# Weight loads begun on GpSimd's DMA queue in place of SyncE's, in a hybrid decoder layer (DeltaNet, dilated window and differential attention, gated FFN)

## The chip, the cores and the metric

The kernel runs on one core of a Trainium2 chip. A core has five engines with an instruction queue each, worked off in order: TensorE (PE in the profile), VectorE (DVE), ScalarE (ACT), GpSimd (POOL) and SyncE (SP). They wait for each other through semaphores. Sixteen DMA engines move data between device memory and the core's own memory; a transfer is begun by an instruction in the queue of one of the engines. The metric is the device time of one execution in microseconds; less is better.

## What is computed

One layer of a decoder over 2048 tokens of width 1024, in float32. Three mixers share one input projection and one output projection, and a gated FFN follows:

```python
h_proj = x @ w_in                      # columns split over the three mixers
y = concat([gated_delta_net(...),      # 4 heads, short causal conv, chunked recurrence
            dilated_window_attn(...),  # 4 heads, three dilation patterns
            diff_attn(...)])           # 4 heads, two softmax maps, causal over all tokens
x = layer_norm(alpha * x + y @ w_out)
gate, val = split(causal_conv3(x @ w_up))          # 1024 -> 2 * 2752
x = layer_norm(alpha * x + (silu(gate) * val) @ w_down)
```

## The kernel before

The tokens are worked in four blocks of 512. For each block there is a projection for the attentions (A0 to A3 in the order lists), one for the DeltaNet (G0 to G3), an attention block of each kind (d0 to d3, w0 to w3), the DeltaNet's chunks (i, b, p, r), and the FFN with the layer norms (t0, f0 to f3). The order of the jobs in the program is set by three lists at lines 1341 to 1343, and the instructions of all of them are then laid out engine by engine by the compiler framework's scheduler, which models when each will be ready. So the queue in which an instruction stands, and its modelled duration, shape the order of everything around it.

Every dense product is done three times in a 32-bit format with shortened mantissas: x and w are each split into a high part and a remainder, and PE sums high times high, high times remainder and remainder times high (lines 182 to 184; 1131 to 1134 for the rows' products, 628 to 630 for the values). A weight tile of 128 x 1024 thus needs two halves, `whi` and `wlo`. `Dense.weights` (line 117) delivers them, from one of two sources:

- **raw**: the tile is loaded (line 130), ACT casts it to the high part (line 132), and POOL subtracts that from the raw tile (line 133). 137 tiles go this way. Where the same weight is needed for later blocks (`keep` is set with job A1), both halves are then stored to device memory (line 137), 101 tiles.
- **ready-made**: a weight that was kept is loaded as its two halves (line 127), 291 times, that is 582 transfers of 512 KB.

All of these tiles, raw ones included, live in one ring of seven 4 KB slots per partition (`NW` at line 1326; the raw tiles of the last block's end have a pool of their own for their halves). A raw weight takes three slots, a ready-made one two. A load may begin when the slot's former user is done: with raw weights, raw tile k+3 takes the slot of remainder k, and remainder k+2 takes that of high part k, both freed by the last matmul of product k.

All transfers of the program, 2035 of them, are begun on SP in one queue: these loads, the stores of the halves, the mixers' loads (keys `ks` at line 709, window tiles at 890 to 917, chunks at 430 to 489) and all results. On POOL stand, besides the subtractions, the mixers' triangular selects (`affine_select`, lines 816 and 411), splits of squares (350, 352) and a scaling (568).

Of the kernel before, what the change touches and what calls it, by code (L numbers as in the profile page):

```python
# [27 lines left out]
def cast(x):  # L28
    return x.bitcast(F32)
# [71 lines left out]
class Dense:  # L101
# [15 lines left out]
    def weights(self, src, k=KD, m=P, pool=None, key=None):  # L117


        nc = self.nc  # L120
        shape = lambda w: w[:, 0 : k * m].rearrange("p (k m) -> p k m", k=k)
        own = lambda dt, name: shape(self.wp.tile([P, 1024], dt, tag="w", name=name, bufs=NW))
        put = lambda name: shape(pool.tile([P, 1024], F32R, tag=name, name=name)) if pool else own(F32R, name)
        if key in self.kept:
            parts = put("whi"), put("wlo")
            for part, d in zip(parts, self.kept[key]):
                nc.sync.dma_start(out=cast(part), in_=cast(shape(d)))
            return parts
        raw = own(F32, "wraw")
        nc.sync.dma_start(out=raw, in_=src)  # L130
        hi, lo = put("whi"), put("wlo")
        nc.scalar.copy(hi, raw)  # L132
        nc.gpsimd.tensor_tensor(out=lo, in0=raw, in1=hi, op=ALU.subtract)  # L133
        if key is not None and self.keep:
            self.kept[key] = [self.tc.dram_tile([P, 1024], F32R, name=name) for name in ("whi_d", "wlo_d")]
            for part, d in zip((hi, lo), self.kept[key]):
                nc.sync.dma_start(out=cast(shape(d)), in_=cast(part))
        return hi, lo
# [21 lines left out]
    def put(self, n, emit):  # L160

        self.later.append([n, emit])
# [1056 lines left out]
class Banks:  # L1219
# [10 lines left out]
    def own(self):  # L1230
        return self.banks[-1]
# [190 lines left out]
```

## Time and profile before

| what | value |
|---|---|
| time, median of 3 executions | 3292.46 us (3285.46 to 3297.71) |
| the profiled execution | 3287.69 us |
| its span, first to last instruction | 3285.8 us |
| mean granted clock of PE | 0.955 |
| moved by DMA | 701 MB, mean 213 GB/s, 64% of the 16 DMA engines' time |
| begun on SP | 2035 transfers, all on hardware queue 1 |
| raw weight loads | 137, of 512 KB |
| ready-made halves | 582 loads, of 512 KB |

The page gives busy time by engine; a stretch is a window of the span, in microseconds from its start, for which the same is asked. The trace does not name tile numbers, so the raw weights are followed by their order: the k-th load, the k-th cast and the k-th subtraction belong together. "Idle before" in a row is the time in which the engine stood still just ahead of the instruction, with the event that ended it. Rows of an engine with a q (SPq, POOLq) are its sequencer's: issues and waits, which do not count as busy.

### The profile page before, as it was taken

What the parts mean: (1) busy time and instruction counts of PE and PEld (TensorE: products, weight loads), DVE (VectorE), ACT (ScalarE), POOL (GpSimd) and SP (SyncE); (2) the same over time, 40 slices, a digit from 0 to 9 for tenths busy, and PEclk for the clock granted to TensorE, in tenths of its full rate; (3) what the DMA queues carried; (4) which work ended last, traced back from release to release, by engine and by line L of the source; (5) the groups of instructions that cost most, each with busy time, mean ns of one, the idle gap of its engine ahead of it and who ended that gap; (6) DMA issues with size and microseconds to landing.
All of it is one profiled execution on the core that took longest, in us unless ns stands there. A gap on an engine that the chain in (4) does not pass through costs nothing.

```text
span 3285.8 us, 41437 instructions
## 1 busy us (share of the span) xinstructions
PE 3039.0 (92%) x14476; PEld 2335.1 (71%) x14476; DVE 1940.7 (59%) x3738; ACT 1251.7 (38%) x2735; POOL 493.0 (15%) x342
## 2 busy tenths in 40 slices
PE   7888687999978888998999999999999999999998
PEld 5666576787767667666776667777788666788887
DVE  2564177858544536755887645565897444474446
ACT  2644143353324315644655422232655333221113
POOL 3452252111102003333312000000000000000001
PEclk8899898999988989999999999999999999999999
DMA  6437776766778878766785655555775444665553
GB/s 190 144 132 263 262 257 218 222 208 200 242 253 276 289 246 265 245 225 209 269 281 198 232 187 177 180 184 173 238 261 201 148 162 144 209 236 192 192 188 139
DMA packets 365281, 701.06 MB, mean 213 GB/s; under 512 B 63024, under 2 KB 189488, under 8 KB 364304
## 3 DMA queue, kind: packets, MB, share of 16 engines
q1 hardware_dynamic: 365072, 698.41, 64.0%
q8 instruction: 115, 1.88, 0.2%
q14 instruction: 94, 0.77, 0.1%
HBM read 525.99 MB, written 172.16 MB: 212 GB/s over the span
## 4 chain that ended last, share of the span: by engine, by line
PE 57%; DMA 7%; DVE 4%; ACT 2%; issue 2%; SPq 1%; POOL 0%; ACTq 0%; POOLq 0%; DVEq 0%
PE d L184 9%; PE d L183 9%; PE d L182 9%; PE rp L1131 6%; PE rp L1132 6%; PE rp L1134 5%; PE bank L791 4%; PE bank L806 2%; DMA wraw<-in_w_up 2%; DMA wlo<-wlo_d 2%; PE bank L970 1%; PE bank L740 1%; PE bank L977 1%; PE bank L931 1%; DMA wraw<-in_w_down 1%
## 5 line engine op out<-in xcount | busy, mean ns | idle before, releaser
L182 PE MATMUL d<-xhi,whi 128*128 128x512 f32 x2144 | 872.4, 408 | 54.7 <-DVE i_halo L336 18.1
L184 PE MATMUL d<-xhi,wlo 128*128 128x512 f32 x2144 | 866.4, 404 | 22.4 <-DMA wlo<-wlo_d 18.2
L183 PE MATMUL d<-xlo,whi 128*128 128x512 f32 x2144 | 864.9, 403 | 1.8 <-DVE xlo L145 1.7
L182 PEld LDWEIGHTS d<-xhi,whi 128*128 128x128 f32 x2144 | 416.9, 195 | 164.0 <-issue 20.3
L133 POOL TENSOR_TENSOR wlo<-wraw,whi 128x1024 fp32r<-128x1024 f32 x137 | 337.1, 2461 | 1207.7 <-ACT whi L132 1067.8
L184 PEld LDWEIGHTS d<-xhi,wlo 128*128 128x128 f32 x2144 | 415.9, 194 | 131.8 <-DMA wlo<-wlo_d 20.4
L183 PEld LDWEIGHTS d<-xlo,whi 128*128 128x128 f32 x2144 | 416.6, 194 | 105.8 <-issue 18.2
L1131 PE MATMUL rp<-whi,hhi 128*128 128x512 f32 x704 | 278.6, 400 | 6.0 <-DVE r L1141 2.3
L1132 PE MATMUL rp<-wlo,hhi 128*128 128x512 f32 x704 | 279.3, 397 | 0.0
L1134 PE MATMUL rp<-whi,hlo 128*128 128x512 f32 x672 | 263.0, 397 | 0.0
L132 ACT CAST whi<-wraw 128x1024 fp32r<-128x1024 f32 x137 | 143.6, 1048 | 281.0 <-DMA wraw<-in_w_gdn 65.2
L749 ACT ACTIVATE bank<-bank,nm 128x512 f32<-128x512 f32 (+3 forms) x320 | 190.3, 595 | 110.8 <-DVE nm L745 72.7
L745 DVE TENSOR_REDUCE nm<-bank 128x1 f32<-128x512 f32 (+3 forms) x288 | 165.4, 596 | 72.6 <-PE bank L740 70.4
L1063 ACT COPY ub<-d 128x512 f32<-128x512 f32 x172 | 100.7, 586 | 265.4 <-PE d L184 264.7
L812 DVE SCALAR_TENSOR_TENSOR pd<-pe,f_nlam,pd 128x512 f32<-128x512 f32 (+3 forms) x160 | 123.5, 786 | 124.4 <-ACT pe L808 81.5
L816 POOL TENSOR_SCALAR_AFFINE_SELECT pd<-pd 128x128 f32<-128x128 f32 x64 | 29.8, 472 | 1018.0 <-DVE pd L812 990.6
L1131 PEld LDWEIGHTS rp<-whi,hhi 128*128 128x128 f32 x704 | 133.2, 189 | 43.4 <-issue 6.3
L1132 PEld LDWEIGHTS rp<-wlo,hhi 128*128 128x128 f32 x704 | 133.3, 189 | 35.0 <-issue 8.5
L1141 DVE TENSOR_TENSOR r<-r,rp 128x512 f32<-128x512 f32 x152 | 102.3, 684 | 84.1 <-PE rp L1134 77.4
L1134 PEld LDWEIGHTS rp<-whi,hlo 128*128 128x128 f32 x672 | 127.0, 189 | 33.0 <-issue 6.5
L1064 DVE COPY c_halo<-d 128x2 f32<-128x2 f32 x172 | 26.8, 156 | 205.2 <-ACT ub L1063 205.0
L1068 DVE SCALAR_TENSOR_TENSOR yg<-ub,c_taps,yg 128x512 f32<-128x512 f32 x176 | 144.8, 823 | 3.6
(280 smaller groups left out, 4723.2 us busy)
## 6 DMA issues: line engine op xcount, KB each, us to landing
whi<-whi_d SPq DMA_DIRECT2D x291, 512.0 KB
wlo<-wlo_d SPq DMA_DIRECT2D x291, 512.0 KB
whi_d<-whi SPq DMA_DIRECT2D x101, 512.0 KB
wlo_d<-wlo SPq DMA_DIRECT2D x101, 512.0 KB
ks<-fk_d SPq DMA_DIRECT2D x160, 196.0 KB
wraw<-in_w_up SPq DMA_DIRECT2D x43, 512.0 KB
wraw<-in_w_gdn SPq DMA_DIRECT2D x32, 512.0 KB
wraw<-in_w_down SPq DMA_DIRECT2D x25, 512.0 KB
```

What stands on the lines that cost most here:

```text
L132: nc.scalar.copy(hi, raw)
L133: nc.gpsimd.tensor_tensor(out=lo, in0=raw, in1=hi, op=ALU.subtract)
L182: nc.tensor.matmul(out=ps, lhsT=whi[:, k], rhs=xhi[k], start=(k == 0), stop=False)
L183: nc.tensor.matmul(out=ps, lhsT=whi[:, k], rhs=xlo[k], start=False, stop=False)
L184: nc.tensor.matmul(out=ps, lhsT=wlo[:, k], rhs=xhi[k], start=False, stop=(k == KD - 1))
L745: nc.vector.tensor_reduce(out=o, in_=s[:, 0:nf], axis=mybir.AxisListType.X, op=ALU.min)
L749: nc.scalar.activation(out=s[:, 0:n], in_=s[:, 0:n], func=AF.Exp, scale=-1.0, bias=o, accum_out=den[:, b, m, qt : qt + 1])
L791: nc.tensor.matmul(out=po[64 * hh : 64 * hh + 64, q0:], lhsT=v[:, 64 * hh : 64 * hh + 64], rhs=pd[hh][:, q0:], start=start, stop=stop)
L1068: nc.vector.scalar_tensor_tensor(out=yc, in0=ub[:, j : j + TB], scalar=self.taps[:, mt, j : j + 1], in1=yc, op0=ALU.mult, op1=ALU.add)
L1131: nc.tensor.matmul(out=ps, lhsT=hi[:, sl], rhs=whi, start=first, stop=False)
L1132: nc.tensor.matmul(out=ps, lhsT=hi[:, sl], rhs=wlo, start=False, stop=last and lo is None)
L1134: nc.tensor.matmul(out=ps, lhsT=lo[:, sl], rhs=whi, start=False, stop=last)
```

## The change

Two lines of `Dense.weights` name another engine as the one that begins the transfer. SP keeps the mixers' loads and all stores, the stores of the halves among them.

```diff
         if key in self.kept:
             parts = put("whi"), put("wlo")
             for part, d in zip(parts, self.kept[key]):
-                nc.sync.dma_start(out=cast(part), in_=cast(shape(d)))
+                nc.gpsimd.dma_start(out=cast(part), in_=cast(shape(d)))
             return parts
         raw = own(F32, "wraw")
-        nc.sync.dma_start(out=raw, in_=src)
+        nc.gpsimd.dma_start(out=raw, in_=src)
```

719 of 2035 transfers thus move from SP's queue to POOL's. The scheduler lays out everything anew; the three places below show what the prediction speaks of.

**SP in f0, before.** In the first block of the FFN all weights are raw. `wraw_14377`, `wraw_14420` and `wraw_14470` are three that follow each other; `whi_d` and `wlo_d` are the stores of the halves, `ks` a key tile of the attention.

```order
L137 DMA whi_d_14333<-whi_14329 128x1024
L130 DMA wraw_14377<-in_w_up 128x1024
L137 DMA wlo_d_14334<-wlo_14330 128x1024
L709 DMA ks_9682<-fk_d_1526 98x512
L137 DMA whi_d_14383<-whi_14379 128x1024
L130 DMA wraw_14420<-in_w_up 128x1024
L137 DMA wlo_d_14384<-wlo_14380 128x1024
L137 DMA whi_d_14426<-whi_14422 128x1024
L130 DMA wraw_14470<-in_w_up 128x1024
```

The next raw load stands behind the store of the high part of the weight ahead of it, which needs ACT's cast, and before the store of its remainder, which needs POOL's subtraction.

**POOL at the same place, now.**

```order
L130 DMA wraw_14377<-in_w_up 128x1024
L133 TENSOR_TENSOR wlo_14380<-wraw_14377,whi_14379 128x1024
L130 DMA wraw_14420<-in_w_up 128x1024
L133 TENSOR_TENSOR wlo_14423<-wraw_14420,whi_14422 128x1024
L130 DMA wraw_14470<-in_w_up 128x1024
L133 TENSOR_TENSOR wlo_14473<-wraw_14470,whi_14472 128x1024
```

Load and subtraction alternate; before, the subtractions stood here by themselves. This holds for all raw weights but the last four, with selects of the mixers in between at places. The load of one weight stands behind the subtraction of the weight ahead of it.

**PE at the same place, from the end of the product of `whi_14422` into that of `whi_14472`.** `d` is a product, `bank` an attention score from keys `ks` and queries `qs`. Before:

```order
L182 MATMUL d_14430<-xhi_10799,whi_14422 128x512
L183 MATMUL d_14430<-xlo_10801,whi_14422 128x512
L184 MATMUL d_14430<-xhi_10799,wlo_14423 128x512
L182 MATMUL d_14480<-xhi_10736,whi_14472 128x512
L183 MATMUL d_14480<-xlo_10738,whi_14472 128x512
L184 MATMUL d_14480<-xhi_10736,wlo_14473 128x512
L740 MATMUL bank3_9025<-ks_9665,qs_9586 128x384
```

Now:

```order
L182 MATMUL d_14430<-xhi_10799,whi_14422 128x512
L740 MATMUL bank1_9023<-ks_9778,qs_9590 128x512
L183 MATMUL d_14430<-xlo_10801,whi_14422 128x512
L184 MATMUL d_14430<-xhi_10799,wlo_14423 128x512
L740 MATMUL bank3_9025<-ks_9757,qs_9590 128x512
L740 MATMUL bank0_9022<-ks_9757,qs_9590 128x512
L740 MATMUL bank2_9024<-ks_9778,qs_9590 128x512
L182 MATMUL d_14480<-xhi_10736,whi_14472 128x512
L183 MATMUL d_14480<-xlo_10738,whi_14472 128x512
L740 MATMUL bank1_9023<-ks_9792,qs_9590 128x512
L740 MATMUL bank3_9025<-ks_9778,qs_9590 128x512
L740 MATMUL bank0_9022<-ks_9778,qs_9590 128x512
```

More of the attention's matmuls now stand between and within the raw products. Counted over all raw weights, PE's matmuls of every kind from the first use of one weight's remainder to that of the next are, on the mean:

| raw weights of | A0 | G0 | A1 | G1 | output projection of block 0 | f0 |
|---|---|---|---|---|---|---|
| how many | 16 | 16 | 12 | 16 | 8 | 65 |
| stretch of the profile before, us | 0:124 | 124:240 | 240:370 | 370:525 | 985:1055 | 1226:1783 |
| matmuls per weight, before | 21.8 | 26.3 | 34.1 | 28.7 | 23.0 | 31.9 |
| matmuls per weight, now | 22.7 | 33.7 | 25.5 | 37.7 | 25.9 | 36.8 |

**POOL among the DeltaNet's chunks, now.** Here the weights come ready-made: `whi` and `wlo` from their stores, between the mixers' select `mq`, scalings `on` and splits `isqh`, `isql`.

```order
L411 AFFINE_SELECT mq_4564<-mq_4564 128x512
L127 DMA wlo_5145<-wlo_d_2384 128x1024
L127 DMA whi_5192<-whi_d_2437 128x1024
L127 DMA wlo_5193<-wlo_d_2438 128x1024
L127 DMA whi_5240<-whi_d_2491 128x1024
L127 DMA wlo_5241<-wlo_d_2492 128x1024
L127 DMA whi_5273<-whi_d_2530 128x1024
L411 AFFINE_SELECT mq_4598<-mq_4598 128x512
L568 TENSOR_TENSOR on_4482<-on_4482,rst_4535 128x512
```

Before, the same loads stood on SP, with the mixers' loads and stores between them:

```order
L127 DMA wlo_5145<-wlo_d_2384 128x1024
L127 DMA whi_5192<-whi_d_2437 128x1024
L345 DMA v_d_4919<-th_5046 128x512
L457 DMA qk_4410<-qk_d_2098 128x8x128
L127 DMA wlo_5193<-wlo_d_2438 128x1024
L127 DMA whi_5240<-whi_d_2491 128x1024
L331 DMA z_d_4920<-th_5092 128x512
L408 DMA mq_4414<-at_d_3670 128x512
```

What a weight load now stands behind is POOL's work for the mixers, and no longer SP's transfers for them.

## The prediction, made before the changed kernel ran

> **What bounds the kernel now.** I read the page's first part, then the table of stretches (cut where the raw weights begin and end), then the rows of the weights, then the waits.
>
> ```profile
> PE 3039.0 (92%) x14476; PEld 2335.1 (71%) x14476; DVE 1940.7 (59%) x3738; ACT 1251.7 (38%) x2735; POOL 493.0 (15%) x342
> ```
>
> ```profile
> core 0: us, PE busy (x) PEld busy (x) DVE busy (x) ACT busy (x) POOL busy (x), PEclk, DMA share, GB/s
> 0.00:124.00 124.00, 90.50 (x318) 67.32 (x318) 39.09 (x127) 54.03 (x118) 41.99 (x28) 0.86 0.61 183
> 124.00:240.00 116.00, 105.62 (x450) 80.70 (x448) 79.35 (x97) 55.09 (x99) 64.57 (x47) 0.95 0.37 116
> 240.00:370.00 130.00, 104.98 (x510) 77.89 (x510) 52.70 (x113) 43.85 (x82) 32.98 (x17) 0.88 0.75 250
> 370.00:525.00 155.00, 126.45 (x539) 101.81 (x539) 93.68 (x143) 52.37 (x111) 62.10 (x39) 0.88 0.80 267
> ...
> 985.00:1055.00 70.00, 62.37 (x435) 51.55 (x433) 35.05 (x69) 27.56 (x65) 20.44 (x11) 0.90 0.79 265
> ...
> 1226.00:1783.00 557.00, 525.18 (x2151) 387.58 (x2150) 384.25 (x682) 304.58 (x669) 168.54 (x83) 0.97 0.74 246
> 1783.00:3226.00 1443.00, 1423.27 (x6408) 1077.54 (x6407) 833.89 (x1599) 476.40 (x1024) 21.84 (x37) 0.99 0.58 194
> ```
>
> PE sets the time: 247 of 3286 us are idle, and only 20 of them lie in 1783 to 3226. The reader is to see that the idle time stands early, and that the first stretches also have the low granted clock (0.86 to 0.95 against 0.99). Six of these stretches hold the raw weights: 16 in each of the first two, 12 and 16 in the next two, 8 in 985:1055, 65 in 1226:1783. They are the ones that are split by ACT and POOL before PE can use them; all other loads bring ready-made halves. This is one weight's way in the last of them, f0:
>
> ```profile
> 1558.97 0.42 SPq L130 DMA_DIRECT2D wraw<-in_w_up  x1
> 1563.70 1.05 ACT L132 CAST whi<-wraw 128x1024 fp32r<-128x1024 f32 x1 [0.43 <-DMA wraw<-in_w_up]
> 1564.83 2.39 POOL L133 TENSOR_TENSOR wlo<-wraw,whi 128x1024 fp32r<-128x1024 f32 x1 [3.76 <-ACT whi L132]
> 1565.15 0.43 SPq L130 DMA_DIRECT2D wraw<-in_w_up  x1
> ```
>
> Load to cast 4.73 us, cast to subtraction 1.13, and the next load goes out 0.32 after the subtraction has **begun**: 6.18 us per weight. What PE needs for one weight is 24 matmuls; where nothing holds it they start this far apart (29 rows, the first and the last):
>
> ```profile
> 3214.61 0.39 PE L184 MATMUL d<-xhi,wlo 128*128 128x512 f32 x1
> 3220.95 0.39 PE L182 MATMUL d<-xhi,whi 128*128 128x512 f32 x1
> ```
>
> 6.34 / 28 = 0.226 us, so 5.43 us a weight. The chain of 6.18 is already a little longer than that; mixer matmuls between the products fill the rest.
>
> **The change part by part.**
>
> *The wait that is added.* On POOL the order is strict: subtraction k, then load k+1 (the order rows in the change). POOL works in order, so the load now starts when the subtraction has **ended**: 2.39 in place of 0.32, +2.07 us. Behind the load stand the next subtraction and the mixers' selects; PE waits for the subtraction in the third matmul of a product.
>
> *The issue itself.* The trace has no DMA begun on POOL. Bounds are the issue on SP and the longest POOL instruction:
>
> ```profile
> L130 SPq DMA_DIRECT2D wraw<-in_w_up x43: 333/383/698, 1226.4 to 1724.6; - x43
> L133 POOL TENSOR_TENSOR wlo<-wraw,whi 128x1024 fp32r<-128x1024 f32 x137 | 337.1, 2461 | 1207.7 <-ACT whi L132 1067.8 <-ACT ub L1062 53.1 <-DMA wlo_d<-wlo 33.1
> L436 POOL MEMSET fx<- 64x1024 f32 x4 | 3.8, 947 | 33.1 <-DMA x_d<-fx 16.9 <-DVE yc L338 10.7 <-DMA y_d<-yb 4.1
> ```
>
> 0.38 to 2.46 us. I take 0.95, the row of a plain POOL instruction that reads nothing, which is what an issue is most like; that is 0.57 over SP's. The chain becomes 6.18 + 2.07 + 0.57 = **8.82 us** in f0. The Trainium skill, "DMA: Bandwidth & Descriptors", section "Latency and other measured facts", puts the first byte of a DMA from GpSimd at about 1 us and of one from Sync at about 0.6. By it the excess would be 0.4 and the chain 8.65, an estimate of 15 us less in all (0.17 x 133 x 2/3); no row here shows either price.
>
> *Raw stretches.* Load to cast differs with the traffic:
>
> ```profile
> 0.81 0.39 SPq L130 DMA_DIRECT2D wraw<-in_w_att  x1
> 4.46 1.04 ACT L132 CAST whi<-wraw 128x1024 fp32r<-128x1024 f32 x1 [2.37 <-DMA wraw<-in_w_att]
> 150.90 0.33 SPq L130 DMA_DIRECT2D wraw<-in_w_gdn  x1
> 155.14 1.05 ACT L132 CAST whi<-wraw 128x1024 fp32r<-128x1024 f32 x1 [3.05 <-DMA wraw<-in_w_gdn]
> 997.95 1.62 SPq L130 DMA_DIRECT2D wraw<-in_w_out  x1
> 1004.72 1.04 ACT L132 CAST whi<-wraw 128x1024 fp32r<-128x1024 f32 x1 [1.78 <-DMA wraw<-in_w_out]
> ```
>
> The chain after is load to cast + 1.13 + 2.39 + 0.57; before it was load to cast + 1.13 + 0.32. For the third, fourth and fifth raw stretch I take 5.5 from load to cast: 6.77 has 1.62 of issue on SP and the stores that are ahead in the same queue, and 4.24 is the traffic of the second. What a product leaves for the chain is PE's own work per raw weight, by the table of matmuls in the change (new order), x 0.226 / the stretch's granted clock. The added wait per weight is the chain after, less the greater of the chain before and that work:
> - 0:124: 7.74 - (22.7 x 0.226 / 0.86 = 5.97) = 1.77, x 16 = 28
> - 124:240: 8.33 - (33.7: 8.02) = 0.31, x 16 = 5
> - 240:370: 9.59 - 6.95 (25.5: 6.55) = 2.64, x 12 = 32
> - 370:525: 37.7: 9.68, over 9.59 = 0
> - 985:1055: 9.59 - 6.95 (25.9: 6.50) = 2.64, x 8 = 21
> - f0: 8.82 - (36.8: 8.57) = 0.25, x 65 = 16
>
> 102 us. But these stretches have 137 us of idle PE now (the spans less the busy times above), from other causes; some of those waits will fall beside the chain's, while uneven filling adds to it. I take two thirds: **+68**. The new order's mixer work is what hides the rest; if it came as in the old order, f0 alone (31.9 matmuls: 7.43) would cost 1.39 x 65 = 90.
>
> *The last block's end.* Four raw weights; in the new order the fourth load stands behind two subtractions (2 x 2.4), and PE has 18 matmuls (4.1 us) ahead of the last: **+4**.
>
> *Ready-made halves, 525 to 985 and from 1783.* Two issues of 0.95 per 5.43 us of PE: hidden; the cover goes when an issue takes over 2.7. But they queue behind the mixers' POOL work:
>
> ```profile
> POOL mq L411 <- ACT mq L410: 140.9, 13, 46.1
> ```
>
> POOL waits 10.8 us at a time for such a select. The ring is two products ahead (10.9 us), so most is hidden, one of 46.1 would not be: **+10**, ends 0 and 35.
>
> *What SP no longer does.*
>
> ```profile
> PE d L184 <- DMA wlo<-wlo_d: 18.2, 5, 7.9
> PE bank L740 <- DMA ks<-fk_d: 14.7, 4, 5.6
> PE vp L629 <- DMA wlo<-wlo_d: 14.6, 4, 4.9
> PE bank L931 <- DMA qw<-wq_d: 9.6, 1, 9.6
> ...
> PE bank L932 <- DMA ql<-wl_d: 0.4, 1, 0.4
> ```
>
> ```profile
> SPq L127 <- PE d L184: 389.0, 118, 9.8
> ```
>
> SP stood 389 us behind line 127, waiting for PE to free a ring slot, with the mixers' loads behind it. All waits of PE for a DMA come to 70 us, in 12 rows from 18.2 to 0.4; 57 of them are in the four rows above. Each would be shorter if the two sorts of load passed each other. But the 14.7 of ks follow a store of the same data, and a weight now has POOL's waits ahead of it in place of SP's: **-25**, ends 0 and -70.
>
> Sum: 68 + 4 + 10 - 25 = +57. The profiled execution took 3287.7 us (span 3285.8); it is 4.8 under the median of 3292.5, inside the runs' spread. 3287.7 + 57 = **3345 us**.
>
> **The rivals.**
> 1. *The load is quick enough, and the two queues free each other: faster.* A weight's load no longer lies behind 512 KB stores in one queue. With 3.65 from issue to cast everywhere, and an issue as short as SP's, the chain is 7.17: 1.2 x 16 = 19 in 0:124, 0.2 x 20 = 4 in 240:370 and 985:1055, nothing elsewhere; two thirds are 15. With 55 of the 70 us of DMA waits gone: 3287.7 + 15 + 4 - 55 = 3252. It decides where the relief is 35 us or more and the chain no longer than this. Against it: 4.73 was measured in f0, the stores still share the engines, and the waits for ks follow a store.
> 2. *The queue does not matter: no change.* The order is made anew, so mixer work may cover the whole shortage: gains and losses of some 40 each, 3288. The same Trainium skill page, section "Rules for kernel authors", says that spreading DMAs over the issuing engines only saves issue time; by that rule this case is the likeliest. The rows speak for it on bandwidth (DMA share 0.37 to 0.80, not full), but it leaves out what waits behind the issue.
> 3. *Issues on POOL are dear: much slower.* At 2.46 every chain is 1.51 longer: 52 + 29 + 50 + 23 + 33 + 114 = 301 in the list above, two thirds 200, so 3287.7 + 200 - 11 = 3477. A milder form: each issue waits for one of DVE's instructions.
>
> ```profile
> L1066 DVE TENSOR_SCALAR yv<-ub,c_taps 128x512 f32<-128x512 f32 x84 | 47.5, 565 | 0.0
> ```
>
> That adds at most 0.57 to a chain, over 133 weights 76, two thirds 51: 3396. The Trainium skill, "SBUF — State Buffer", section "SBUF: two separate sides", has such a lock: DVE in a two-port mode keeps GpSimd from writing descriptors. Nothing in this trace shows one, since no DMA starts on POOL.
>
> **How the numbers follow.** Forecast (3310 to 3400) 0.52; rival 1 0.20; rival 2 0.21; rival 3 0.07. About 0.5% (16 us) is what a measurement can tell from no change. Faster 0.20, same 0.21, slower 0.59. The range leaves out most of rival 3 and the better half of rival 1: 3255 to 3425; an issue of 1.5 us (+0.55 a chain, as with the milder form) ends inside it.
>
> **What would show it.** In the profile after: the next raw load on POOL begins at or after the end of the subtraction, and f0's subtractions stand 8 to 9 us apart where PE has no mixer work; an issue row on POOL near 1 us; POOL busy or issuing 1100 us or more; more idle PE before `wlo` of POOL and `whi` of ACT in 124:525 and in f0; fewer waits for wlo_d, ks and qw. It is wrong if subtractions stand 7 us apart or less, if an issue takes over 2 us, or if PE's idle time moves in the stretches without raw weights.

## The result, and the profile after

| | median, us | spread, us | profiled span, us | granted clock |
|---|---|---|---|---|
| before | 3288.96 | 3277.03 to 3297.71 | 3285.8 | 0.955 |
| after | 3411.91 | 3410.46 to 3414.80 | 3408.6 | 0.947 |

The ratio is 1.0387, with an interval of 1.0358 to 1.0415: slower, by 127 us on a scale of 3289 (118 to 136). 3345 was forecast, +57, so the side was right and the size less than half. Below, a "price" is always the ratio less one, times 3289.

First the busy line of the page after; it stands against the first line of the prediction.

```profile
PE 3077.2 (90%) x14476; PEld 2345.0 (69%) x14476; DVE 1931.5 (57%) x3738; ACT 1254.1 (37%) x2733; POOL 877.6 (26%) x1061
```

PE does the same 14476 matmuls. Its idle time grew from 247 to 331 us (3408.6 - 3077.2), and the same matmuls were busy 38 us longer, at a lower clock. 85 + 38 is the whole difference of the spans. Now the stretches of the profile after, cut near the first raw load of the next:

```profile
0.00:166.00 166.00, 103.02 (x346) 74.49 (x346) 41.64 (x135) 60.66 (x134) 54.04 (x52) 0.83 0.44 137
166.00:305.00 139.00, 128.58 (x581) 96.72 (x582) 89.29 (x150) 62.51 (x114) 68.55 (x56) 0.93 0.40 130
305.00:445.00 140.00, 102.23 (x398) 72.62 (x397) 29.17 (x52) 32.75 (x52) 42.50 (x37) 0.82 0.77 250
445.00:618.00 173.00, 139.04 (x775) 109.55 (x775) 111.47 (x181) 57.68 (x122) 68.31 (x60) 0.90 0.63 208
...
1322.00:2022.00 700.00, 634.61 (x2575) 440.67 (x2576) 435.34 (x831) 365.85 (x782) 218.72 (x184) 0.95 0.65 214
2022.00:3351.00 1329.00, 1322.43 (x5956) 1027.24 (x5955) 775.62 (x1448) 418.86 (x912) 239.81 (x428) 1.00 0.59 201
```

93 us are lost by the end of G1 (618 against 525), all of it in stretches of raw weights. But the stretches do not hold the same work: 0:305 has 927 matmuls where 0:240 had 768, and f0 has 2575 where it had 2151; what came early in f0 is missing from 2022:3351, which is 114 us shorter than its counterpart. The scheduler drew mixer work forward into the gaps, so a stretch that grew is not yet a price. For that the parts had to be run by themselves.

This is POOL in f0, after (start, duration, instruction, idle time ahead of it):

```profile
1646.49 2.36 POOL L133 TENSOR_TENSOR wlo<-wraw,whi 128x1024 fp32r<-128x1024 f32 x1 [6.03 <-ACT whi L132]
1648.81 0.57 POOL L130 DMA_DIRECT2D wraw<-in_w_up  x1
1655.65 2.34 POOL L133 TENSOR_TENSOR wlo<-wraw,whi 128x1024 fp32r<-128x1024 f32 x1 [6.28 <-ACT whi L132]
```

and the cast between the two, on ACT:

```profile
1654.53 1.03 ACT L132 CAST whi<-wraw 128x1024 fp32r<-128x1024 f32 x1
```

The load begins when the subtraction ends (1646.49 + 2.36), occupies POOL for 0.57 us, and the cast follows 5.72 us after the load began; 1.12 later the next subtraction: 9.16 us a weight (median over f0 9.23). The mechanism of the forecast is there, row by row. PE pays for it in its waits for the raw weights' halves, first before, then after:

```profile
PE d L182 <- ACT whi L132: 13.0, 4, 5.9
PE d L184 <- POOL wlo L133: 4.0, 4, 1.8
```

```profile
PE d L182 <- ACT whi L132: 39.9, 25, 7.2
PE d L184 <- POOL wlo L133: 28.2, 22, 2.6
```

With the same waits at the other lines it is 41 us before and 109 after, 68 of the 85 us of added idle time.

### The profile page after: what moved, and what is told of

Its sections match the earlier page's. It is cut to its first block, busy times and chain, and to the rows that moved or that the text cites. A ratio compares the mean times of both kernels' runs of the same rounds, so it can differ in the third digit from the quotient of the medians.

```text
span 3408.6 us, 41550 instructions
## 1 busy us (share of the span) xinstructions
PE 3077.2 (90%) x14476; PEld 2345.0 (69%) x14476; DVE 1931.5 (57%) x3738; ACT 1254.1 (37%) x2733; POOL 877.6 (26%) x1061
## 5 line engine op out<-in xcount | busy, mean ns | idle before, releaser
L133 POOL TENSOR_TENSOR wlo<-wraw,whi 128x1024 fp32r<-128x1024 f32 x137 | 327.1, 2388 | 778.1 <-ACT whi L132 658.3
L127 POOL DMA_DIRECT2D wlo<-wlo_d x291 | 157.0, 539 | 1342.3 <-PE d L184 704.7
L1131 PE MATMUL rp<-whi,hhi 128*128 128x512 f32 x704 | 271.5, 400 | 6.3 <-ACT whi L132 5.4
L127 POOL DMA_DIRECT2D whi<-whi_d x291 | 166.8, 573 | 21.0 <-PE rp L1134 7.0
L740 PE MATMUL bank<-ks,qs 96*128 96x512 f32 (+3 forms) x320 | 111.2, 393 | 48.1 <-DMA ks<-fk_d 25.1
```

Source lines behind the costliest of these rows:

```text
L127: nc.gpsimd.dma_start(out=cast(part), in_=cast(shape(d)))
L740: nc.tensor.matmul(out=s[:, 0:n], lhsT=qs[0:96, m, qt * P : (qt + 1) * P], rhs=ks[0:96, 0, 0:n], start=True, stop=True)
L1131: nc.tensor.matmul(out=ps, lhsT=hi[:, sl], rhs=whi, start=first, stop=False)
```

## The experiments

### Which of the two lines costs it

The halves alone on POOL (`e1_halves_pool`), and the raw loads alone (`e2_raw_pool`), each with the other line as before:

```diff
 # e1, against the changed kernel
-        nc.gpsimd.dma_start(out=raw, in_=src)
+        nc.sync.dma_start(out=raw, in_=src)
 # e2, against the changed kernel
-                nc.gpsimd.dma_start(out=cast(part), in_=cast(shape(d)))
+                nc.sync.dma_start(out=cast(part), in_=cast(shape(d)))
```

> Only the ready-made halves are begun on POOL; the 137 raw weights' loads stand on SyncE as before. Theory (the cost is that a raw load on POOL stands behind the subtraction of the weight before): the chain per raw weight is back at 6.2 us in the first feed-forward block, and the time is 3250 to 3295 us, no slower than before. Rival A (the software queue itself is the slower path, whatever stands ahead of it): 582 of the 719 loads still use it, so most of the loss stays, 3360 us or more. Rival B (the mixers' own loads come later because POOL's and SyncE's loads now compete): the first 525 us stay as before, since the halves are hardly used there, and the loss shows later, over 3310 us.

> Only the raw weights' loads are begun on POOL; the ready-made halves stay on SyncE. Theory (raw load behind the subtraction): the whole loss is here, the first 525 us grow by some 90 us as in the changed kernel, 3390 to 3430 us. Rival A (software queue slow as such): 137 of 719 loads, so a fifth of the loss, about 3315 us. Rival B (competition of mixers' loads with halves): under 3320 us.

| run | ratio | interval | price, us |
|---|---|---|---|
| halves alone | 1.0063 | 1.0039 to 1.0087 | +21 |
| raw loads alone | 1.0245 | 1.0218 to 1.0271 | +81 |
| both (the change) | 1.0387 | 1.0358 to 1.0415 | +127 |

137 loads cost four times what 582 cost, so it is no price per load on that queue. The raw loads fell short of the 3390 us expected (3367.65), and the halves cost 21 us where the theory expected no loss. That is near rival B of the halves' run (its first 525 us unchanged, over 3310 us in all; 3289 + 21 = 3310 here), to which the halves' section comes back. The two alone leave 25 us of the whole unexplained, with an uncertainty of some 15.

### The place in the order, or the queue

Four kernels leave the number and size of all loads as they are, and free the raw load from this weight's work, and a fifth is a control. Two ways: the raw load of the next weight is issued ahead of this weight's cast and subtraction (`e4` with all loads on POOL, `e7` with the halves on SP, `e5` with all loads on SP), or the subtraction goes to VectorE (`e3` with all loads on POOL, and `e3b` with all on SP as the control).

```diff
 # e4, e7, e5 (the engine of the two loads differs)
+        ahead, self.ahead = self.ahead, None
+        raw = load(src, k, m) if ahead is None else ahead[1]
...
+                nxt = self.order[0][0]
+                self.ahead = nxt, load(*raw_source(self.I, nxt))
         hi, lo = put("whi"), put("wlo")
         nc.scalar.copy(hi, raw)
         nc.gpsimd.tensor_tensor(out=lo, in0=raw, in1=hi, op=ALU.subtract)
 # e3, e3b
-        nc.gpsimd.tensor_tensor(out=lo, in0=raw, in1=hi, op=ALU.subtract)
+        nc.vector.tensor_tensor(out=lo, in0=raw, in1=hi, op=ALU.subtract)
```

> The changed kernel, but within a run of raw weights the next weight's raw load is issued on POOL ahead of this weight's subtraction; same queue, same number of loads. Theory: the load no longer waits for a subtraction, the period per raw weight in the first feed-forward block falls from about 9.1 us to 6 or less, and the time falls by 80 us or more from the changed kernel's 3412, to 3260 to 3330 us. Rival A (the queue as such): stays at 3390 or more. Rival B (a raw weight's buffer is what is short, 7 in the pool): the load goes early in the order but waits for a buffer, period 7.5 to 9 us, 3350 to 3400 us.

> As the prefetch on POOL (raw load of the next weight issued ahead of this weight's subtraction), but the ready-made halves stay on SyncE. Theory (halves behind the mixers' POOL work cost some 20 us, as in the run with the halves alone; raw loads gain by their place): 3205 to 3235 us, below the 3239 of the prefetch with the halves on POOL. Rival (halves and raw loads must share a queue, or the mixers' loads suffer from the halves on SyncE): 3240 to 3280 us.

> All loads on SyncE as in the kernel before; only the next raw load is issued ahead of this weight's cast, store and subtraction. Theory (place in the order decides, not the queue): as good as on POOL, 3215 to 3255 us. Rival A (the gain of the prefetch on POOL comes from a queue without SyncE's stores): 3270 us or more.

> The changed kernel with the subtraction of the raw weights on VectorE; all 719 loads stay on POOL's queue. Theory (the load waits for the subtraction ahead of it in POOL's order): the next load no longer waits for it, the loss of the first 525 us goes, and the time is 3280 us or less, with VectorE some 150 us busier. Rival A (queue as such): 3390 us or more. Rival B (VectorE is too late for the subtractions, it is at 57 to 60%): the load goes early but the subtraction starts 2 us or more after the cast, 3320 to 3380 us.

> The control for the run before: the kernel before with the subtraction on VectorE and all loads on SyncE. What the move of the subtraction is worth by itself. Theory: the load stands behind the store of the high part here, not behind the subtraction, so little changes: within 25 us of the kernel before, 3255 to 3305 us, and the changed kernel's loss of some 125 us has no counterpart between this run and the one with POOL's queue (they differ by under 40 us). Rival A: they differ by 100 us or more, as the two kernels of the case do.

| run | loads begun on | ratio | interval | price, us |
|---|---|---|---|---|
| `e4`, load ahead | POOL, all | 0.9851 | 0.9823 to 0.9879 | -49 |
| `e7`, load ahead | POOL, raw only | 0.9832 | 0.9812 to 0.9853 | -55 |
| `e5`, load ahead | SP, all | 0.9832 | 0.9805 to 0.9859 | -55 |
| `e3`, subtraction on VectorE | POOL, all | 0.9824 | 0.9804 to 0.9844 | -58 |
| `e3b`, subtraction on VectorE | SP, all | 0.9891 | 0.9867 to 0.9915 | -36 |

With the load issued ahead the three choices of queue cannot be told apart, and all are faster than the kernel before. From the changed kernel to `e4`, one statement's place takes away 176 us on the same queue with the same transfers. POOL in `e4`, in f0 (the code that was put in moves the raw load to line 160 and the subtraction to 174):

```profile
1503.39 2.38 POOL L174 TENSOR_TENSOR wlo<-wraw,whi 128x1024 fp32r<-128x1024 f32 x1 [1.60 <-PE rp L1173]
...
1505.97 0.58 POOL L160 DMA_DIRECT2D wraw<-in_w_up  x1
...
1510.79 2.38 POOL L174 TENSOR_TENSOR wlo<-wraw,whi 128x1024 fp32r<-128x1024 f32 x1 [0.50 <-PE rp L1173]
```

The load that goes out at 1505.97 belongs to a later weight than the subtraction at 1510.79, and the subtractions stand 7.4 us apart (median over f0 7.34). Of f0's 65 subtractions 20 are released by the cast, where it was 54 in the changed kernel. The time was better than the 3260 to 3330 us expected, and the period longer than the 6 us. PE's idle time in this execution is that of the kernel before (3228.4 - 2983.2 = 245); its gain is busy time of the same matmuls, 56 us, at a clock of 0.967 in place of 0.955, which by itself makes 38. But these two executions stand at the ends of what their kernels show (0.961 to 0.967, and 0.955 to 0.964 before), so how the 49 us divide between waits and clock is not settled. `e7` was expected below `e4` by the price of the halves; the two cannot be told apart. `e3` and `e3b` are 22 us apart with intervals that do not touch: without a subtraction in its queue POOL is the better place. That SP's stores of the halves stand ahead of the raw loads there would be a reason; it was not tried by itself. The VectorE runs change one thing more. `e3` was expected to make VectorE some 150 us busier, and it was 29 busier than in the changed kernel (1960.3 against 1931.5), since what VectorE does beside a subtraction on POOL takes longer (see the last section). So their gain may not be the free load's alone: `e3b`, where the load still stands behind the store of the high part, has 36 us of it.

### What a microsecond of the chain is worth

Two runs change the subtraction of the changed kernel: done twice on POOL (`e6_sub_twice`), and split in two halves that run on POOL and VectorE at once (`e11_sub_half`).

```diff
 # e6
         nc.gpsimd.tensor_tensor(out=lo, in0=raw, in1=hi, op=ALU.subtract)
+        nc.gpsimd.tensor_tensor(out=lo, in0=raw, in1=hi, op=ALU.subtract)
 # e11
-        nc.gpsimd.tensor_tensor(out=lo, in0=raw, in1=hi, op=ALU.subtract)
+        for eng, a in ((nc.gpsimd, slice(0, k // 2)), (nc.vector, slice(k // 2, k))):
+            eng.tensor_tensor(out=lo[:, a], in0=raw[:, a], in1=hi[:, a], op=ALU.subtract)
```

> The changed kernel with every raw weight's subtraction on POOL done twice in a row (same result), 2.39 us more between two raw loads. Theory: the stretches of raw weights are paced by load, cast and subtraction in a row, so 137 times up to 2.4 us is added to the chain, of which PE's work covers what is left: period in the first feed-forward block about 11.5 us, time 3480 to 3590 us. Rival A or B (POOL is at 26% busy and the subtraction is not in the way): under 20 us is added, at most 3435 us.

> The changed kernel with half of each subtraction on POOL and half on VectorE at the same time (same result): POOL is 1.2 us shorter between two raw loads. Theory (no threshold of PE's work: each us of the chain costs what it cost in the run with two subtractions, about 120 us for 2.4 us): 55 to 70 us faster than the changed kernel, 3335 to 3360 us on the scale of 3289 before. Rival (the prediction's cover, where only A0, A1 and the output projection are paced by the chain): about 43 us faster at two thirds, 3365 to 3375 us. Rival B (the loss sits in the queue): under 15 us faster.

`e6` came to 1.0752 (1.0714 to 1.0789), 3530 us, the number expected, but it was not the test it was meant to be. POOL in f0:

```profile
1695.51 2.70 POOL L133 TENSOR_TENSOR wlo<-wraw,whi 128x1024 fp32r<-128x1024 f32 x1 [2.73 <-ACT whi L132]
1698.17 0.57 POOL L130 DMA_DIRECT2D wraw<-in_w_up  x1
1698.76 2.35 POOL L134 TENSOR_TENSOR wlo<-wraw,whi 128x1024 fp32r<-128x1024 f32 x1
```

The scheduler put the next load between the two subtractions. The chain from load to load hardly grew (median in f0 9.68 us, 9.29 in the changed kernel; about 11.5 was expected); what came 2.9 us later was the remainder for PE. So it prices a remainder that is 2.9 us later (120 us over the changed kernel), together with what the added subtractions cost VectorE (see the last section), and tells nothing about the length of the chain. POOL in `e11`, in f0, and all 137 of its halves (shortest, median, longest in ns):

```profile
1633.68 1.28 POOL L134 TENSOR_TENSOR wlo<-wraw,whi 128x512 fp32r<-128x512 f32 x1 [6.78 <-ACT whi L132]
...
L134 POOL TENSOR_TENSOR wlo<-wraw,whi x137: 1256/1757/1857, 8.5 to 3330.7; 128x512 fp32r<-128x512 f32 x137
```

The row has one of the short ones: the mean is 1.60 us, against 2.39 for a whole subtraction in the changed kernel. So the chain is 0.79 us shorter, not the 1.2 of the expectation, and the ratio is 1.0257 (1.0223 to 1.0290), a price of 85 against 127. 0.79 x 133 weights = 105 us less chain gave back 42, good to some 14: PE's work does cover a good part. The time is in the rival's range, 3365 to 3375, and not in the theory's, 3335 to 3360. But both were worked out for 1.2 us. For 0.79 the theory's 120 us per 2.4 makes 40, and the prediction's list, at two thirds, 33. The run does not tell them apart. The remainder is also complete 0.55 us sooner after the cast (median 2.96 for 3.51), which would have a price of its own.

### Where the raw loads cost it

`e13_raw_pool_a0g0` begins only the 32 raw loads of A0 and G0 on POOL, `e14_raw_pool_a1g1` only the 28 of A1 and G1, and `e18_after_a0g0_sp` is the changed kernel with the first 32 on SP again.

```diff
 # e13, against the kernel before
-        nc.sync.dma_start(out=raw, in_=src)
+        (nc.sync if self.keep else nc.gpsimd).dma_start(out=raw, in_=src)
 # e14, against the kernel before
-        nc.sync.dma_start(out=raw, in_=src)
+        early = self.keep and key and key[0] in ("att", "val", "gdn")
+        (nc.gpsimd if early else nc.sync).dma_start(out=raw, in_=src)
 # e18, against the changed kernel
-        nc.gpsimd.dma_start(out=raw, in_=src)
+        (nc.gpsimd if self.keep else nc.sync).dma_start(out=raw, in_=src)
```

> Only the 32 raw loads of the first two projections (A0 and G0, before any half is stored) are begun on POOL; everything else on SyncE as before. Theory (no halves are stored here, so before the change SyncE began these loads several us ahead; that lead is lost on POOL, and PE's work covers little of it): 40 to 60 us slower than the kernel before. Rival (the prediction's reckoning: PE's work per weight covers nearly all in G0, 28 + 5 us, two thirds of it): 15 to 30 us slower.

> Only the 28 raw loads of the next two projections (A1 and G1, whose halves are stored) are begun on POOL. Theory (PE's work per weight does not cover the chain in G1): 28 times some 1.2 us, 25 to 45 us slower, most of it in G1. Rival (the prediction's reckoning: 32 us in A1 of which two thirds, none in G1 since 37.7 matmuls cover the chain): 21 us, all of it in A1.

> The changed kernel, but the 32 raw loads of A0 and G0 are begun on SyncE again. Theory (these 32 hold more than half of the raw loads' price, and their loss at the start is carried to the end unchanged): 45 to 75 us faster than the changed kernel, 52 to 82 us slower than the kernel before. Rival (the parts alone add up to less than the whole because of an interplay with the halves' loads later, not in A0 and G0): the same 55 us come off, so 72 us slower than before. Rival B (the new order made for the whole matters, not these 32): under 30 us come off.

| run | ratio | interval | price, us |
|---|---|---|---|
| A0 and G0 alone, 32 loads | 1.0168 | 1.0144 to 1.0192 | +55 |
| A1 and G1 alone, 28 loads | 1.0029 | 1.0015 to 1.0043 | +10 |
| the change without A0 and G0 | 1.0218 | 1.0196 to 1.0240 | +72 |

55 us are in the first 32 weights, alone as within the whole (127 - 72), and most of it in A0: from the first raw load of A0 to that of G0 it takes 116.9 us before and 161.5 in `e13`, from there to that of A1 121.8 and 134.1. Before, nothing was stored yet in A0, and SP ran ahead: in the median the next load went out 1.56 us before the subtraction began, where it now goes out 2.31 after. SP there, before, and POOL beside it:

```profile
93.37 0.84 SPq L130 DMA_DIRECT2D wraw<-in_w_val  x2
```

```profile
94.06 2.35 POOL L133 TENSOR_TENSOR wlo<-wraw,whi 128x1024 fp32r<-128x1024 f32 x1 [10.55 <-ACT whi L132]
```

Two raw loads had gone out before one subtraction began. After, in A0, load by load behind the subtraction, on POOL:

```profile
96.07 2.35 POOL L133 TENSOR_TENSOR wlo<-wraw,whi 128x1024 fp32r<-128x1024 f32 x1 [9.40 <-ACT whi L132]
98.37 0.57 POOL L130 DMA_DIRECT2D wraw<-in_w_val  x1
107.17 2.33 POOL L133 TENSOR_TENSOR wlo<-wraw,whi 128x1024 fp32r<-128x1024 f32 x1 [8.23 <-ACT whi L132]
```

A0 and G0 in `e13`, up to the first cast of A1, and what follows:

```profile
0.00:304.00 304.00, 230.77 (x938) 170.11 (x939) 133.18 (x290) 123.40 (x251) 123.78 (x107) 0.89 0.44 136
304.00:3342.00 3038.00, 2822.49 (x13539) 2164.44 (x13538) 1809.53 (x3449) 1126.29 (x2486) 380.95 (x267) 0.96 0.65 217
```

The same before, with the stretches of G1 and of the ready-made weights behind it:

```profile
0.00:245.00 245.00, 200.66 (x777) 151.60 (x778) 122.18 (x229) 109.75 (x218) 108.42 (x75) 0.90 0.50 154
...
398.00:525.00 127.00, 106.19 (x461) 86.04 (x459) 93.68 (x143) 50.76 (x109) 61.53 (x37) 0.89 0.75 253
525.00:996.00 471.00, 421.47 (x2810) 353.06 (x2811) 303.23 (x658) 172.64 (x451) 67.11 (x78) 0.93 0.71 225
```

A0 and G0 take 59 us longer, and all that follows takes 3038 us in place of 3041 (3286 - 245), although 161 matmuls fewer were left for it: the mixer work that was drawn forward did not shorten what follows.

`e14` missed both expectations. Its G1 grew as in the changed kernel, yet the time was given back. G1 in `e14`, and the stretch behind it:

```profile
401.00:569.00 168.00, 133.24 (x754) 105.10 (x754) 105.90 (x182) 57.73 (x122) 67.34 (x57) 0.90 0.62 201
569.00:1010.00 441.00, 401.79 (x2537) 332.97 (x2537) 292.94 (x620) 167.83 (x440) 65.00 (x74) 0.95 0.74 237
```

G1 is 41 us longer with 293 matmuls more, and the stretch behind it 30 us shorter with 273 fewer: here the work drawn forward did pay. By difference, the output projection, f0 and the last block hold 81 - 55 - 10 = 16 us when the raw loads move alone.

### Where the halves cost it

`e16_halves_pool_mixers` begins only the halves of the mixers' projections on POOL, 136 of 582 loads, and `e17_halves_pool_ffn` only the other 446. All else is as before.

```diff
-                nc.sync.dma_start(out=cast(part), in_=cast(shape(d)))
+                (nc.gpsimd if key[0] in ("att", "val", "gdn") else nc.sync).dma_start(out=cast(part), in_=cast(shape(d)))
 # e17: ("out", "up", "down", "end")
```

> Only the ready-made halves of the mixers' projections (blocks 2 and 3) are begun on POOL; the halves of the output projection and of the FFN, and all raw loads, stay on SyncE. Theory (a half waits on POOL for PE to free a ring slot, and the DeltaNet's selects, splits and scalings stand behind it; the mixers' loads on SyncE come no sooner for it): the whole price of the halves is here, 15 to 30 us slower than the kernel before. Rival (the price is that of the queue, spread over all halves): about a fifth of it, under 8 us.

> The counterpart: only the ready-made halves of the output projection and of the FFN are begun on POOL. Theory (POOL has little other work there): within 8 us of the kernel before. Rival (queue): most of the 21 us of the run with all halves, 13 us or more slower.

`e16`: 1.0064 (1.0044 to 1.0083), +21 us, the whole price of the halves. `e17`: 0.9995 (0.9979 to 1.0010), nothing. Of the 21 us, the largest single piece is one hole of PE among the DeltaNet's chunks. PE in `e16`:

```profile
994.20 1.09 PE L468 MATMUL kp<-d_ident,qk 128*128 128x128 f32 x4 [14.38 <-DMA qk<-qk_d]
```

SP in `e16` ahead of it, where the load of `qk` is at line 457:

```profile
964.99 8.53 SPq L673 DMA_DIRECT2D fk_d<-sy  x3
973.62 5.75 SPq L457 DMA_DIRECT2D qk<-qk_d  x1
979.46 9.52 SPq L446 DMA_DIRECT2D x_d<-fx  x1
```

And SP before; by its place in the order (the last of 16) the `qk` load is the same:

```profile
947.14 2.69 SPq L446 DMA_DIRECT2D x_d<-fx  x1
...
973.52 0.58 SPq L457 DMA_DIRECT2D qk<-qk_d  x1
```

The load is begun at the same time, but PE used it 4.6 us later before and 20.6 us later in `e16`. The order on SP is another: `x_d` stood ahead of this load and now stands behind it, and three stores of keys are right ahead of it. And the two queues run side by side. This is what each moved from 965 to 990 in `e16` (packets, MB, share of the 16 DMA engines' time; q0 is POOL's, q1 SP's):

```profile
q0 software_dynamic: 1429, 5.20, 57.1%
q1 hardware_dynamic: 1445, 1.79, 19.8%
```

In 945 to 970 before, SP's queue moved 5.97 MB, and POOL's nothing. The three stores and the load are 1.31 MB: an estimate is 18 us at the rate of 1.79 MB in 25 us, and 5.5 at the rate of 5.97. So the halves, no longer in one queue with the mixers' transfers, take most of the DMA engines' time, and the data that PE waits for is late. That is the competition which rival B of the halves' run named. How much of it is the new order alone was not tried. Before, line 468 waited for `qk` three times, 4.1 us in all. The same hole, 13.6 and 14.5 us, is in `e1` and in the changed kernel; in `e17`, where the mixers' halves stay on SP, the longest wait of line 468 for `qk` is 1.7 us. That the scalings and selects of the mixers stand behind halves on POOL, as expected, is the lesser part here: the waits of line 571 for the scaled rows go from 5.2 to 8.9 us.

### Both remedies

`e9_prefetch_dve` is `e4` with the subtraction on VectorE.

> Both remedies together: the next raw load issued ahead on POOL's queue, and the subtraction on VectorE. Theory (either alone frees the load, so the second adds only the shorter subtraction, 1.23 against 2.4 us): 3205 to 3235 us. Rival (what now limits is a free slot in the ring of seven, or PE itself): no gain on 3230 to 3240 us.

0.9746 (0.9722 to 0.9770), 3204.5 us against 3286.2: 84 us faster than the kernel before and the fastest of all. That is half a microsecond below the range expected; the second remedy adds 26 us to `e3` and 35 to `e4`.

## Why the prediction was half right

- **The added wait: right.** The load begins at the end of the subtraction, and the kernels that free it are 176 us (`e4`) and more faster than the changed one. Its size of 2.07 us was read from one weight; over f0 the next load went out 0.77 us (median) after the subtraction began before, and 2.33 after, so 1.56 were added.
- **The issue on POOL: too dear.** 0.95 was taken, the rows show 0.57. The chain in f0 is 9.16, not 8.82, all the same, because load to cast rose from 4.73 to 5.72. POOL is busy 878 us, not the 1100 or more that were to show it.
- **Raw stretches and the last block: +72 forecast, +81 measured (72 to 89) for the raw loads alone.** The sum was near by luck, for its terms were not, and the factor of two thirds had no row behind it. A0 and G0 were set at 33 x 2/3 = 22 and cost 55; the rest was set at 50 and cost 26. In these two stretches two things failed. In A0, load to cast was taken as 3.65 us from the first load of the program, when nothing else moved; over the 15 later loads of A0 its median after is 6.05 (before it was 6.19, so the profile before already had it), and 6.05 + 1.13 + 2.35 = 9.53 is the period there (median 9.49; 7.74 was forecast). And PE's work in the new order (33.7 matmuls a weight in G0, where 26.3 had stood) was counted as cover, but matmuls drawn forward count only if they shorten what comes later, which they did not there. A1 and G1 are the other way round: 21 forecast, all in A1, and 10 measured, since G1, for which nothing was forecast, grew by 41 us and 30 came back behind it.
- **Halves +10 and relief of SP -25: the step that failed.** Together -15 were forecast, +21 were measured: 36 of the 70 us by which the sum of 57 fell short (9 are the raw loads', 25 the next point's). The waits that were to go did go: for `wlo_d` and `whi_d` PE waited 34.0 us before and now 6.4. But the mixers' loads came later, not sooner. PE's waits in the changed kernel (total, times, longest):

```profile
PE bank L740 <- DMA ks<-fk_d: 25.1, 3, 12.2
PE kp L468 <- DMA qk<-qk_d: 16.2, 2, 14.5
PE t1p L498 <- DMA g_xlow<-x_d: 12.1, 6, 2.8
...
PE vp L629 <- DMA wlo<-wlo_d: 4.5, 4, 1.6
PE d L184 <- DMA wlo<-wlo_d: 1.0, 1, 1.0
PE vp L628 <- DMA whi<-whi_d: 0.9, 1, 0.9
```

  The first three were 14.7, 4.1 and 0.9 before. All waits of PE for a DMA were 70 us before and are 75 after, so nothing was relieved. The sum had it that the two sorts of load would pass each other; it left out that the halves on a queue of their own take DMA time from the mixers' loads (57% against 20% in the hole of `e16`).
- **The rest, 25 us (some 15 either way),** belongs to the two moves together, and the sum had no term for it. It lies behind G0: without A0 and G0 the change costs 72, of which the parts alone explain 21 + 26. What makes it there is not settled.
- **Rival 1** (the queues free each other) fell with the halves. **Rival 2** fell as well: the order was made anew, but did not cover the shortage. The Trainium skill, "DMA: Bandwidth & Descriptors", section "Rules for kernel authors", which stood behind it, is borne out where the load's place is free (`e5` and `e7` have the same ratio, with SP and with POOL). Where the load stands behind the work that uses the load before it, the place costs what no queue does. **Rival 3** fell with 0.57 us an issue. Its milder form shows in no row either: the longest of the 719 issues on POOL takes 0.96 us, and f0's raw loads land 5.2 us (median) after their begin where VectorE does little beside the issue and 5.4 where it is busy for most of it.

## What to carry to other kernels

A load that is moved to another engine's queue is moved behind that engine's instructions. Look up what stands ahead of it there: where it is the consumer of the previous load, the two become one chain, and issuing the next load ahead of that consumer, or giving the consumer to another engine, was worth more here than any choice of queue. Price the start of a program by itself, with load times from a busy row, for there is no other work yet that could fill a gap. And a queue that is relieved of some loads does not simply run sooner: those loads now run beside it, and what was in time can come late.

## What was not expected of the hardware

Single issues can hold SP for long: 12.81 us for `x_d` in the changed kernel (9.52 in `e16`), where the longest issue of the kernel before is 4.3. What makes them long is open. They are not only found where SP was relieved: in `e3b`, with all loads on SP, the longest is 7.09, and in `e17`, with 446 loads fewer on it, 4.38.

A subtraction on POOL holds up VectorE. This one starts on VectorE while POOL's subtraction of 1646.49 still runs:

```profile
1647.78 1.62 DVE L1093 TENSOR_TENSOR hlo<-yv,hhi 128x512 fp32r<-128x512 f32 x1
```

In the changed kernel the median of line 1093's `hlo` is 2.29 us where it overlaps a subtraction (9 of them) and 0.69 elsewhere. VectorE's same 3738 instructions were busy 1931.5 us there and 2123.2 in `e6`, where POOL subtracts twice. Summed over all its instructions that overlap work of POOL, VectorE took 163 us more than the same instructions do elsewhere in the changed kernel, and 40 in `e3`. What this is worth in the kernel's time was not tried by itself.

The granted clock is lower where PE idles longer, but not by idle time alone: 0.936 in `e6` (441 us idle), 0.947 in the changed kernel (331), 0.965 in `e3` (222), yet 0.955 before and 0.967 in `e4`, which idle alike (247 and 245). In the changed kernel the same matmuls took 38 us longer, nearly a third of the loss; the ratio of the clocks (0.955 to 0.947) makes 26 of them. The prediction had left the clock as it was. The Trainium skill, "TensorE: Matmul & The Clock Gate", section "Part 1: The HAM clock gate", says that the clock falls to half after an idle window of about 3.4 us. The hole of PE in the changed kernel (14.52 us without a matmul, up to 1060.47) agrees; PEclk is the third number from the end:

```profile
1050.00:1060.00 10.00, 0.00 (x0) 0.00 (x0) 0.00 (x0) 1.22 (x2) 0.00 (x0) 0.50 0.68 251
1060.00:1064.00 4.00, 3.53 (x13) 3.18 (x14) 0.69 (x1) 3.33 (x7) 0.00 (x0) 0.50 0.26 64
```

The clock is at half in the hole, stays there for the first matmuls behind it, and is 0.93 in 1064:1080. By stretches it is 0.83 where PE idled 63 of 166 us, and 1.00 in 2022:3351 where it idled 7 of 1329.
